# Down projection by seven block products, in three passes, with block additions on GpSimd

## The chip, the cores and the metric

The kernel runs on one core of one Trainium2 chip. The metric is the time of one execution in device microseconds (us). One execution in which every instruction was recorded (the profiled execution) gives the page, the groups and the time lines that are quoted. In the profile PE is the matrix engine (TensorE), PEld its weight loads, DVE is VectorE, ACT is ScalarE, POOL is GpSimd and SP is SyncE, which issues the DMAs here. PSUM is the memory into which PE writes its sums; it has eight banks of 128 partitions by 512 fp32 numbers.

## The reference

Two layers over 512 tokens of width 1024. Layer 0 mixes tokens by differential attention, layer 1 by gated linear attention (GLA), both beside a cross-attention into 256 memory tokens. Each layer ends in a gated MLP with a causal convolution of width 3 between its two projections, and this MLP is the part that the change rewrites:

```python
def conv_ffn(h, w_up, conv_w, conv_b, w_down):
    u = h @ w_up                       # 512 x 1024 by 1024 x 5632
    c = conv(u, width 3, causal, per column) + conv_b
    a, g = jnp.split(c, 2, axis=-1)
    return (jax.nn.silu(g) * a) @ w_down   # 512 x 2816 by 2816 x 1024

for i in range(DEPTH):                 # DEPTH = 2
    ...
    h = rms_norm(x, ffn_norm[i])
    x = x + conv_ffn(h, w_up[i], conv_w[i], conv_b[i], w_down[i])
```

## The kernel before

**Layout and precision.** Tokens are held transposed: `xT[k]` is one of eight tiles of 128 model columns by 512 tokens. A product in fp32 accuracy is made of three products in a faster format: each operand is split into a high part (ACT copies it, rounding) and a low part (DVE subtracts the high part), and PE sums high x high, high x low and low x high. `xh`, `xl` are the two parts of the tokens, `whi`, `wlo` those of the weights, `midh`, `midl` (or `xsh`, `xsl` in the buffers of the pool `xs`) those of the MLP's hidden tiles.

**Weights.** The host packs all weights into blocks of 128 x 1024 numbers in the order of their use. SP loads them through three `raw` buffers; `make_block` and `split_weights` (lines 251 and 254) split each into `whi` and `wlo`, of which there are six buffers (`WB`). `weights(key)` returns a piece's parts, and makes blocks up to two pieces ahead.

**The MLP.** `ffn` goes through the 11 groups of hidden columns (q, 256 columns of each half) in two passes, `HALVES = (6, 5)`. In a pass, `up` forms for every q four products (gate and value, two 128-column tiles of each), each of 24 matmuls of 512 tokens, in four PSUM banks with the tags mm and sm (two banks to a tag). The tokens are not yet divided by their root mean square there: the factor `rB` is found by `row_scales` while the first products run, and `conv` multiplies each product by it on DVE (line 1126), then applies the convolution with one ACT and two DVE instructions (1128 to 1130). Silu, a product and the split of the hidden tile follow (1161 to 1165). At the end of a pass, four steps c follow, each with the down projection for two output tiles, 2c and 2c+1: 36 or 30 matmuls of 512 tokens to a tile, in one bank of tag lg and one of tag tp. `update` adds the bank to `xT` (line 1074), and in layer 0's last pass makes the next layer's operands at once (line 309 on DVE, 308 on ACT) and sums up their squares (421, 423).

**Order.** PE's order is written by hand. The orders of the other engines are set by a scheduler when the program is built; each engine then takes its instructions strictly in that order, and waits on semaphores. The first projection of layer 1 (`gemm` with the key `gm`, lines 328 to 330) follows the last down projection of layer 0 on PE. It opens its first two sums in banks with the tag mm.

Of the kernel before, what the change touches and what calls it, by code (L numbers as in the profile page):

```python
# [21 lines left out]
S = 512  # L22
# [8 lines left out]
HALVES = (6, 5)  # L31
# [147 lines left out]
def trunk(ctx, tc, head_d, x_t, mem_t, wpack, cols_a_d, cols_d, conv_d, gate_d, rel_bias, diff_lambda, consts, onehot, out):  # L179
# [93 lines left out]

    def make_block(raws=None):
# [9 lines left out]
        hi, lo = (wp.tile([128, WTILE], F32R, name=t, tag=t, bufs=WB) for t in ("whi", "wlo"))  # L284
        split_weights(slice(0, n * w), raw, hi, lo, i == 2)
        made[i] += [(hi[:, blk(j, w)], lo[:, blk(j, w)]) for j in range(n)]
# [3 lines left out]
    used = [0]  # L290
# [820 lines left out]
    def ffn(pool, l, acc):  # L1111
        rB = pool.tile([128, S], F32, name="rB", bufs=1)
        us = [pool.tile([128, S + 128], F32, name=f"u{i}", bufs=1)[:, :S + 2] for i in range(4)]
        for u in us:
            G.memset(u[:, 0:2], 0.0)
        nu = [0]

        def up(parts, n):
            i = nu[0]
            nu[0] += 1  # L1120
            p = bank("mm" if i % 4 < 2 else "sm")
            product(p, parts, n, list(zip(xh, xl)))
            return p, us[i % 4]

        def conv(p, u, j):
            V.tensor_mul(u[:, 2:], p, rB)  # L1126
            c = pool.tile([128, S], F32, name="cvo", bufs=6)
            A.activation(c, u[:, 2:], AF.Identity, scale=cv[l][:, 2, j:j + 1], bias=cv[l][:, 3, j:j + 1])  # L1128
            V.scalar_tensor_tensor(c, u[:, 1:S + 1], cv[l][:, 1, j:j + 1], c, op0=ALU.mult, op1=ALU.add)  # L1129
            V.scalar_tensor_tensor(c, u[:, 0:S], cv[l][:, 0, j:j + 1], c, op0=ALU.mult, op1=ALU.add)  # L1130
            return c
# [15 lines left out]
        base = 0  # L1147
        for half, nq in enumerate(HALVES):
            mids = []
            for q in range(base, base + nq):  # L1150
                wa = weights(("ua", l, q))
                wg = None
                for n in range(2):
                    ua = up(wa, n)
                    wg = wg or weights(("ug", l, q))
                    ug = up(wg, n)
                    if q == 0 and n == 0:
                        row_scales(acc[0])
                    ca = conv(*ua, 2 * q + n)
                    cg = conv(*ug, 22 + 2 * q + n)  # L1160
                    A.activation(cg, cg, AF.Silu)
                    V.tensor_mul(ca, ca, cg)
                    mh, ml = split_tiles() if len(mids) < 5 else split_tiles(pool, "mid", 18)
                    A.copy(mh, ca)
                    V.tensor_sub(ml, ca, mh.bitcast(F32))
                    mids.append((mh, ml))
            last = half == 1
            if last and l == 0:
                tables("natural_log_exp_and_others")
            acc2 = [None]  # L1170
            for c in range(4):
                if last and l == 0 and c == 0:
                    gw = gate_raw[0] = pool.tile([128, S], F32, name="cvo", bufs=6)[:96, :384]
                    G.memset(gw, 0.0)
                    for b in range(3):
                        load(gw[32 * b:32 * b + 17], gate_d)
                pn = bank("lg"), bank("tp")
                parts = weights(("dn", l, base, c))
                final = last and l == 1 and c == 3
                for n in range(2):  # L1180
                    cut = len(parts) - 2 if final and n else len(parts)
                    product(pn[n], parts[:cut], n, mids)
# [102 lines left out]
```

## Time and profile before

| | us |
|---|---|
| time, median of 3 executions | 1163.88 |
| lowest and highest of the 3 | 1163.66, 1164.11 |
| time of the profiled execution | 1163.96 |
| its span, first to last instruction | 1162.2 |
| of the span: up and down stages of layer 0's MLP, about | 250 to 600 |
| of the span: up and down stages of layer 1's MLP, about | 808 to 1162 |

The span is 1.8 us shorter than the time of the same execution, since the time also holds what lies around the first and the last instruction. A matmul's record (389 ns for 512 tokens) is its way from its first input to its last output; matmuls overlap, so a matmul's price is the distance from its start to the next one's start. In the rows, `out<-in` names what is written and read, `xN` is a count, and a row of a group ends with the busy time, the mean length of one in ns, and the engine's idle time just ahead of them, with what ended that.

### The profile page before, as it was taken

What the parts mean: (1) busy time and instruction counts of PE and PEld (TensorE: products, weight loads), DVE (VectorE), ACT (ScalarE), POOL (GpSimd) and SP (SyncE); (2) the same over time, 40 slices, a digit from 0 to 9 for tenths busy, and PEclk for the clock granted to TensorE, in tenths of its full rate; (3) what the DMA queues carried; (4) which work ended last, traced back from release to release, by engine and by line L of the source; (5) the groups of instructions that cost most, each with busy time, mean ns of one, the idle gap of its engine ahead of it and who ended that gap; (6) DMA issues with size and microseconds to landing.
All of it is one profiled execution on the core that took longest, in us unless ns stands there. A gap on an engine that the chain in (4) does not pass through costs nothing.

```text
span 1162.2 us, 14796 instructions
## 1 busy us (share of the span) xinstructions
PE 1157.9 (100%) x5654; PEld 965.8 (83%) x5654; DVE 753.3 (65%) x1262; ACT 545.0 (47%) x951; POOL 6.5 (1%) x30
## 2 busy tenths in 40 slices
PE   9999999999999999999999999999999999999998
PEld 7888887888888888888888888988888888888887
DVE  8676778688677326677457737867976733576741
ACT  6677686555354213354337634436544421344420
POOL 0000000000000000000000000000000000000000
PEclk9999999999999999999999999999999999999999
DMA  8522242233223223222341320332332323232221
GB/s 295 166 82 83 78 144 70 73 108 128 73 93 125 88 80 124 73 98 94 121 146 66 98 96 8 119 112 104 106 112 73 106 94 109 88 112 73 90 101 45
DMA packets 39652, 117.70 MB, mean 101 GB/s; under 512 B 4767, under 2 KB 7256, under 8 KB 39582
## 3 DMA queue, kind: packets, MB, share of 16 engines
q1 hardware_dynamic: 39150, 116.37, 29.8%
q8 instruction: 44, 0.72, 0.3%
q10 hardware_dynamic: 432, 0.39, 0.1%
q14 instruction: 26, 0.21, 0.1%
HBM read 112.54 MB, written 4.21 MB: 100 GB/s over the span
## 4 chain that ended last, share of the span: by engine, by line
PE 99%; DMA 0%; DVE 0%; ACT 0%; issue 0%
PE ps_mm L350 9%; PE ps_mm L349 9%; PE ps_mm L351 9%; PE ps_sm L350 8%; PE ps_sm L351 8%; PE ps_sm L349 8%; PE ps_mm L328 6%; PE ps_mm L330 6%; PE ps_mm L329 6%; PE ps_lg L350 3%; PE ps_lg L351 3%; PE ps_lg L349 3%; PE ps_tp L350 3%; PE ps_tp L351 3%; PE ps_tp L349 3%; PE ps_tp L218 3%
## 5 line engine op out<-in xcount | busy, mean ns | idle before, releaser
L251 ACT CAST whi<-raw 128x1024 fp32r<-128x1024 f32 (+4 forms) x212 | 207.8, 986 | 257.1 <-PE ps_tp L350 120.9
L254 DVE TENSOR_TENSOR wlo<-raw,whi 128x1024 fp32r<-128x1024 f32 (+4 forms) x212 | 240.4, 1139 | 125.8 <-ACT whi L251 125.0
L349 PE MATMUL ps_mm<-xsh,whi 128*128 128x512 f32 x438 | 171.5, 392 | 0.0
L350 PE MATMUL ps_mm<-xsl,whi 128*128 128x512 f32 x438 | 170.6, 389 | 0.0
L351 PE MATMUL ps_mm<-xsh,wlo 128*128 128x512 f32 x438 | 170.5, 389 | 0.0
L349 PE MATMUL ps_sm<-xsh,whi 128*128 128x512 f32 x378 | 147.0, 389 | 0.0
L350 PE MATMUL ps_sm<-xsl,whi 128*128 128x512 f32 x378 | 147.0, 389 | 0.0
L351 PE MATMUL ps_sm<-xsh,wlo 128*128 128x512 f32 x378 | 147.0, 389 | 0.0
L328 PE MATMUL ps_mm<-whi,xsh 128*128 128x512 f32 (+2 forms) x328 | 126.4, 385 | 0.0
L1128 ACT ACTIVATE cvo<-u,cv 128x512 f32<-128x512 f32 x88 | 71.4, 815 | 111.8 <-DVE u L1126 111.8
L330 PE MATMUL ps_mm<-whi,xsl 128*128 128x512 f32 (+2 forms) x328 | 123.0, 375 | 0.0
L329 PE MATMUL ps_mm<-wlo,xsh 128*128 128x512 f32 (+2 forms) x328 | 122.8, 374 | 0.0
L349 PEld LDWEIGHTS ps_mm<-xsh,whi 128*128 128x128 f32 x438 | 82.2, 188 | 17.2 <-issue 0.3
L350 PEld LDWEIGHTS ps_mm<-xsl,whi 128*128 128x128 f32 x438 | 82.3, 188 | 17.1 <-DVE xsl L309 0.4
L351 PEld LDWEIGHTS ps_mm<-xsh,wlo 128*128 128x128 f32 x438 | 82.2, 188 | 17.1
L1129 DVE SCALAR_TENSOR_TENSOR cvo<-u,cv,cvo 128x512 f32<-128x512 f32 x88 | 65.7, 748 | 36.2 <-ACT cvo L1128 36.0
L349 PEld LDWEIGHTS ps_sm<-xsh,whi 128*128 128x128 f32 x378 | 71.0, 188 | 14.8
L350 PEld LDWEIGHTS ps_sm<-xsl,whi 128*128 128x128 f32 x378 | 71.0, 188 | 14.7
L351 PEld LDWEIGHTS ps_sm<-xsh,wlo 128*128 128x128 f32 x378 | 71.0, 188 | 14.6
L328 PEld LDWEIGHTS ps_mm<-whi,xsh 128*128 128x128 f32 x328 | 61.7, 188 | 11.5 <-issue 1.0
L330 PEld LDWEIGHTS ps_mm<-whi,xsl 128*128 128x128 f32 x328 | 61.7, 188 | 11.4
L329 PEld LDWEIGHTS ps_mm<-wlo,xsh 128*128 128x128 f32 x328 | 61.8, 188 | 10.0
(325 smaller groups left out, 1779.2 us busy)
## 6 DMA issues: line engine op xcount, KB each, us to landing
raw<-in_wpack_dram SPq DMA_DIRECT2D x178, 512.0 KB, 3.4
xt<-in_x_t_dram SPq DMA_DIRECT2D x15, 256.0 KB, 5.3
raw<-in_wpack_dram SPq DMA_DIRECT2D x15, 256.0 KB, 5.3
raw<-in_wpack_dram SPq DMA_DIRECT2D x8, 384.0 KB, 3.8
xres<-xt SPq DMA_DIRECT2D x8, 256.0 KB, 3.0
xt<-xres SPq DMA_DIRECT2D x8, 256.0 KB, 5.5
out_dram<-xt SPq DMA_DIRECT2D x7, 256.0 KB, 2.0
bt<-bias_d SPq DMA_DIRECT2D x6, 256.0 KB, 4.6
```

The costliest lines, as they stand in the source:

```text
L218: nc.tensor.transpose(dst, src, ident[:n, :n])
L251: ins = A.copy(hi[:, c], raw[:, c])
L254: V.tensor_sub(lo[:, c], raw[:, c], hi[:, c].bitcast(F32))
L328: mm(p, sh[k][:, blk(b)], hi, start=k == 0, stop=False)
L329: mm(p, sh[k][:, blk(b)], lo, start=False, stop=False)
L330: mm(p, sl[k][:, blk(b)], hi, start=False, stop=k == KT - 1)
L349: mm(p, hi[:, blk(n)], bh, start=i == first, stop=False)
L350: mm(p, hi[:, blk(n)], bl, start=False, stop=False)
L351: mm(p, lo[:, blk(n)], bh, start=False, stop=i == last)
L1128: A.activation(c, u[:, 2:], AF.Identity, scale=cv[l][:, 2, j:j + 1], bias=cv[l][:, 3, j:j + 1])
L1129: V.scalar_tensor_tensor(c, u[:, 1:S + 1], cv[l][:, 1, j:j + 1], c, op0=ALU.mult, op1=ALU.add)
```

## The change

The down projection is done by Strassen's scheme (in the form of Winograd). Two hidden tiles, two output tiles and two halves of the tokens make a 2 x 2 by 2 x 2 product of blocks, for which 7 block products do in place of 8. Each is of 128 x 128 weights by 256 tokens, with the three parts as before. For this, sums of weight blocks (`combined`, four additions to a block of weights) and sums of token halves (`combine`, four additions to a q) are formed on GpSimd (`ADD = G`) and split by ACT and DVE as the plain ones are; the seven products go to four banks, and `decode` puts the output tiles together from them on DVE. The passes become three, of 4, 4 and 3 groups q. Two steps c hold all eight banks in turn: one step has the tags mm and sm, the next lg and tp. From the third group on (q >= 2), the up projection reads tokens that are already scaled (`scaled_tokens`: on DVE, ACT and DVE, eight tiles, once in a layer), so that the multiplication by `rB` falls away, and ACT and DVE read the convolution's input from PSUM. The up stage takes its banks over all four tags (`TURNS`).

```diff
-HALVES = (6, 5)
+HALVES = (4, 4, 3)
+TURNS = ('mm', 'mm', 'sm', 'sm', 'lg', 'lg', 'tp', 'tp')
...
+    def combined(raw, n):
...
+        ADD.tensor_add(s1, a21, a22)
+        ADD.tensor_sub(s3, a11, a21)
+        ADD.tensor_sub(s2, s1, a11)
+        ADD.tensor_sub(s4, a12, s2)
+        A.copy(full(h0)[:, :, :3], r[:, :, :3])
+        V.tensor_sub(full(l0)[:, :, :3], r[:, :, :3], full(h0)[:, :, :3].bitcast(F32))
+        m = slice(0, 512 * pairs)
+        A.copy(h1[:, m], wsum[:, m])
+        V.tensor_sub(l1[:, m], wsum[:, m], h1[:, m].bitcast(F32))
...
+    ADD = G
...
+        if i + 1 < len(plan) and plan[i + 1][0][0] == "dn":
+            limit = first_of[i + 1] + 1
...
-        def conv(p, u, j):
-            V.tensor_mul(u[:, 2:], p, rB)
-            c = pool.tile([128, S], F32, name="cvo", bufs=6)
-            A.activation(c, u[:, 2:], AF.Identity, scale=cv[l][:, 2, j:j + 1], bias=cv[l][:, 3, j:j + 1])
...
+        def conv(p, j, scaled):
+            if not scaled:
+                u = ctile()
+                V.tensor_mul(u, p, rB)
+                p = u
+            c = ctile()
+            A.activation(c, p, AF.Identity, scale=cv[l][:, 2, j:j + 1], bias=cv[l][:, 3, j:j + 1])
+            V.scalar_tensor_tensor(c[:, 1:], p[:, :S - 1], cv[l][:, 1, j:j + 1], c[:, 1:], op0=ALU.mult, op1=ALU.add)
+            V.scalar_tensor_tensor(c[:, 2:], p[:, :S - 2], cv[l][:, 0, j:j + 1], c[:, 2:], op0=ALU.mult, op1=ALU.add)
...
+        def scaled_tokens():
+            out = []
+            for k in range(KT):
+                t = ctile()
+                V.scalar_tensor_tensor(t, xT[k], c_ffn(l, k), rB, op0=ALU.mult, op1=ALU.mult)
+                hi, lo = split_tiles()
+                A.copy(hi, t)
+                V.tensor_sub(lo, t, hi.bitcast(F32))
+                out.append((hi, lo))
+            return out
...
+        def combine(b2, b1):
+            t12, t34 = ctile(), ctile()
+            ADD.tensor_sub(t12[:, left], b1[:, right], b1[:, left])
+            ADD.tensor_sub(t12[:, right], b2[:, right], t12[:, left])
+            ADD.tensor_sub(t34[:, left], b2[:, right], b1[:, right])
+            ADD.tensor_sub(t34[:, right], b2[:, left], t12[:, right])
+            h, lo, m = (mid_tile(), mid_tile()), (mid_tile(), mid_tile()), mid_tile()
+            parts_of(b1[:, left], m[:, left], m[:, right])
+            for t, hi, lw in zip((t12, t34), h, lo):
+                parts_of(t, hi, lw)
...
+        def down(base, nq, mids, tags, last, acc2):
...
+            two = 2 if nq == 4 else 1
+            seq = [(0, m) for m in range(nq - 1)] + [(1, m) for m in range(two)] + [(0, nq - 1)]
+            seq += [(1, m) for m in range(two, nq)] + [(c, m) for c in (2, 3) for m in range(nq)]
...
+                ta, tb = (("mm", "sm"), ("lg", "tp"))[(c + tags) % 2]
+                banks[c] = [bank(t) for t in (ta, ta, tb, tb)]
...
+                for t, (w, v) in enumerate(((hi, bh), (hi, bl), (lo, bh))):
+                    mm(banks[c][b][:, h], w, v, start=b not in seen[c], stop=m == nq - 1 and t == 2 and i in close)
...
+            def decode(c):
+                n1, n2, b = 2 * c, 2 * c + 1, banks[c]
+                u = ctile()
+                x1, x2 = xT[n1], xT[n2]
+                A.copy(u[:, left], b[2][:, left])
+                V.tensor_add(x1[:, left], x1[:, left], b[2][:, left])
+                V.tensor_add(u[:, left], u[:, left], b[2][:, right])
+                V.tensor_add(u[:, right], u[:, left], b[1][:, right])
+                V.tensor_add(u[:, left], u[:, left], b[3][:, left])
+                V.tensor_add(x1[:, right], x1[:, right], u[:, right])
+                x2v = x2.rearrange("p (h c) -> p h c", h=2)
+                V.tensor_add(x2v, x2v, u[:, left].unsqueeze(1).to_broadcast([128, 2, 256]))
...
+                x1, x2, b = decode(c)
+                V.tensor_add(x2, x2, b[1])
+                finish_tile(2 * c + 1)
...
+                    V.tensor_add(x1, x1, b[0])
+                    finish_tile(2 * c)
...
+            for q in range(base, base + nq):
+                if q == 2:
+                    tokens = fresh
...
+                if q == 0:
+                    fresh = scaled_tokens()
```

The orders below are those of the built programs. Line numbers in the rows of the change are those of the changed kernel.

**PE, at the border of the layers.** The end of layer 0's last down projection (lines 349 to 351 before, 1257 in the change) and the start of layer 1's first projection (328 to 330 before, 364 to 366 in the change; `128x272` is its width). Before:

```order
L349 MATMUL ps_tp<-midh,whi 128x512
L350 MATMUL ps_tp<-midl,whi 128x512
L351 MATMUL ps_tp<-midh,wlo 128x512
L328 MATMUL ps_mm<-whi,xsh 128x272
L329 MATMUL ps_mm<-wlo,xsh 128x272
```

And in the change:

```order
L1257 MATMUL ps_sm<-mid,whi 128x256 x2
L1257 MATMUL ps_sm<-mid,wlo 128x256
L1257 MATMUL ps_mm<-mid,whi 128x256 x2
L1257 MATMUL ps_mm<-mid,wlo 128x256
L364 MATMUL ps_mm<-whi,xsh 128x272
L365 MATMUL ps_mm<-wlo,xsh 128x272
```

The last sums of layer 0 moved from the banks lg and tp to mm and sm, so that layer 1's first sum asks for a bank that the last step of the down projection has just filled.

**DVE, at the same place.** Before, the last step's two additions to `xT` (1074), each with the low part (309) and the squares (423) of a next operand, and low parts of weights (254):

```order
L1074 TENSOR_TENSOR xt<-xt,ps_lg 128x512
L309 SCALAR_TENSOR_TENSOR xsl<-xt,cols_a,xsh 128x512
L423 TENSOR_TENSOR xt<-xt 128x512
L254 TENSOR_TENSOR wlo<-raw,whi 128x1024 x2
L1074 TENSOR_TENSOR xt<-xt,ps_tp 128x512
L254 TENSOR_TENSOR wlo<-raw,whi 128x1024
```

In the change, from the step before the last (banks lg and tp) to the last one (mm and sm); 1265 to 1271 are `decode`, 1313 and 1306 the additions behind it, 345 and 459 the next operand and its squares, 257 low parts of weights:

```order
L1313 TENSOR_TENSOR xt<-xt,ps_lg 128x512
L1306 TENSOR_TENSOR xt<-xt,ps_lg 128x512
L257 TENSOR_TENSOR wlo<-raw,whi 128x1024
L345 SCALAR_TENSOR_TENSOR xsl<-xt,cols_a,xsh 128x512
L459 TENSOR_TENSOR xt<-xt 128x512
L345 SCALAR_TENSOR_TENSOR xsl<-xt,cols_a,xsh 128x512
L459 TENSOR_TENSOR xt<-xt 128x512
L257 TENSOR_TENSOR wlo<-raw,whi 128x1024
L1265 TENSOR_TENSOR xt<-xt,ps_sm 128x256
L1266 TENSOR_TENSOR cvo<-cvo,ps_sm 128x256
L1267 TENSOR_TENSOR cvo<-cvo,ps_mm 128x256
L1268 TENSOR_TENSOR cvo<-cvo,ps_sm 128x256
```

A step now has eight additions on DVE in place of two, the step before it and two blocks of layer 1's weights stand ahead of the last step's, and the bank mm is read last (line 1313 of the last step, a few rows further on).

**DVE, between the first and the third group q of a layer.** Before, the work of one q after another:

```order
L254 TENSOR_TENSOR wlo<-raw,whi 128x1024
L1162 TENSOR_TENSOR cvo<-cvo 128x512
L1126 TENSOR_TENSOR u_2662<-ps_sm,rB 128x512
L254 TENSOR_TENSOR wlo<-raw,whi 128x1024
L1165 TENSOR_TENSOR xsl<-cvo,xsh 128x512
```

In the change, with the scaled tokens (1192) and their low parts (1195), and the multiplications by `rB` of q = 1 (1166):

```order
L1192 SCALAR_TENSOR_TENSOR cvo<-xt,cols,rB 128x512
L1195 TENSOR_TENSOR xsl<-cvo,xsh 128x512
L1192 SCALAR_TENSOR_TENSOR cvo<-xt,cols,rB 128x512
L1166 TENSOR_TENSOR cvo<-ps_lg,rB 128x512
L1195 TENSOR_TENSOR xsl<-cvo,xsh 128x512
L1166 TENSOR_TENSOR cvo<-ps_lg,rB 128x512
L1195 TENSOR_TENSOR xsl<-cvo,xsh 128x512
L1170 SCALAR_TENSOR_TENSOR cvo<-cvo,cv_81 128x511
L257 TENSOR_TENSOR wlo<-raw,whi 128x1024
```

Sixteen instructions for the scaled tokens now stand ahead of most of q = 1's work and of the low parts of the weights of q = 2 (line 257).

More of the change, by code (lines that the diff above doesn't have):

```diff
@@ L283, in make_block @@
             made.append([])
-        hi, lo = (wp.tile([128, WTILE], F32R, name=t, tag=t, bufs=WB) for t in ("whi", "wlo"))
-        split_weights(slice(0, n * w), raw, hi, lo, i == 2)
-        made[i] += [(hi[:, blk(j, w)], lo[:, blk(j, w)]) for j in range(n)]
+        if plan[i][0][0] == "dn":
+            made[i] += combined(raw, n)
+        else:
+            hi, lo = (wp.tile([128, WTILE], F32R, name=t, tag=t, bufs=WB) for t in ("whi", "wlo"))
+            split_weights(slice(0, n * w), raw, hi, lo, i == 2)
+            made[i] += [(hi[:, blk(j, w)], lo[:, blk(j, w)]) for j in range(n)]
         if raws is None:
             ahead()
-    used = [0]
+    used, sum_pool = [0], [None]
+    ADD = G
     def weights(key, by_block=False):
@@ L1197, in ffn @@
+                gw = gate_raw[0] = ctile()[:96, :384]
+                G.memset(gw, 0.0)
+                for b in range(3):
+                    load(gw[32 * b:32 * b + 17], gate_d)
+            down(base, nq, mids, nu[0] // 4 % 2, last, acc2)
             base += nq
```

160 lines of the change are left out of this document (111 added, 49 removed).

## The prediction

> **What bounds the kernel now.** The page comes first: busy shares, the granted clock, the chain of waits.
>
> ```profile
> span 1162.2 us, 14796 instructions
> PE 1157.9 (100%) x5654; PEld 965.8 (83%) x5654; DVE 753.3 (65%) x1262; ACT 545.0 (47%) x951; POOL 6.5 (1%) x30
> ...
> PEclk9999999999999999999999999999999999999999
> ...
> PE 99%; DMA 0%; DVE 0%; ACT 0%; issue 0%
> ```
>
> PE ends nearly everything: the chain is 99% PE, and PE is never long without a matmul. So a matmul taken away is time gained, at once, and any wait of PE is time lost, at once; DVE and ACT count only where they make PE wait. How much room they have is read stage by stage, in the busy time by windows: the first and the second group q of layer 0's up stage, then a quarter of a down stage (columns: window, its length, then busy time and count of PE, PEld, DVE, ACT, POOL).
>
> ```profile
> 251.50:273.20 21.70, 21.70 (x97) 18.00 (x96) 19.47 (x27) 12.81 (x16) 0.00 (x0) 1.00 0.28 97
> 273.20:294.90 21.70, 21.70 (x97) 17.96 (x97) 16.02 (x21) 9.65 (x12) 0.00 (x0) 1.00 0.29 98
> 388.50:405.00 16.50, 16.50 (x75) 13.65 (x74) 5.14 (x6) 3.34 (x4) 0.00 (x0) 1.00 0.28 95
> ```
>
> DVE has 2.2 us left in the first q, 5.7 in the next, and two thirds of the down stage. The change puts its additions into that room.
>
> **What the change takes from PE.** The down projection is these groups by form, of line 349, and as many of 350 and 351:
>
> ```profile
> L349 PE MATMUL ps_lg<-midh,whi 128*128 128x512 f32 x96 | 37.4, 389 | 0.0
> L349 PE MATMUL ps_tp<-midh,whi 128*128 128x512 f32 x94 | 36.6, 389 | 0.0
> L349 PE MATMUL ps_lg<-xsh,whi 128*128 128x512 f32 x80 | 31.1, 389 | 0.0
> L349 PE MATMUL ps_tp<-xsh,whi 128*128 128x512 f32 x80 | 31.1, 389 | 0.0
> ```
>
> That is 3 x 350 = 1050 matmuls of 512 tokens, and 12 of 256 at the very end. The distance of starts comes from the time line, the first and the last of 42 in a row of 512 tokens, and of 22 in a row of 256:
>
> ```profile
> 1147.87 0.39 PE L349 MATMUL ps_lg<-xsh,whi 128*128 128x512 f32 x1
> ...
> 1157.16 0.39 PE L351 MATMUL ps_tp<-midh,wlo 128*128 128x512 f32 x1
> ```
>
> ```profile
> 738.74 0.28 PE L330 MATMUL ps_mm<-whi,xsl 128*128 128x256 f32 x1
> ...
> 741.25 0.28 PE L330 MATMUL ps_mm<-whi,xsl 128*128 128x256 f32 x1
> ```
>
> 9.29 us / 41 = 0.2266 and 2.51 / 21 = 0.1195, so a half-width matmul costs 53% of a full one. Before: 1050 x 0.2266 + 12 x 0.1195 = 239.4 us. After: 11 pairs of hidden tiles x 4 pairs of output tiles x 7 products x 3 parts x 2 layers = 1848 matmuls, x 0.1195 = 220.8. **Gain 18.6 us**, not the eighth (30 us) that seven for eight suggests.
>
> **What DVE is given.** Its prices, by form (the mean in ns is the second number behind the bar):
>
> ```profile
> L254 DVE TENSOR_TENSOR wlo<-raw,whi 128x1024 fp32r<-128x1024 f32 x178 | 216.7, 1222 | 120.1 <-ACT whi L251 119.4
> L254 DVE TENSOR_TENSOR wlo<-raw,whi 128x816 fp32r<-128x816 f32 x2 | 2.0, 1009 | 2.3 <-ACT whi L251 2.3
> L254 DVE TENSOR_TENSOR wlo<-raw,whi 128x768 fp32r<-128x768 f32 x8 | 7.5, 953 | 1.0 <-ACT whi L251 1.0
> L254 DVE TENSOR_TENSOR wlo<-raw,whi 128x512 fp32r<-128x512 f32 x15 | 10.3, 685 | 0.0
> L254 DVE TENSOR_TENSOR wlo<-raw,whi 128x256 fp32r<-128x256 f32 x8 | 3.3, 418 | 2.3 <-ACT whi L251 2.2
> L309 DVE SCALAR_TENSOR_TENSOR xsl<-xt,cols_a,xsh 128x512 fp32r<-128x512 f32 x8 | 6.0, 750 | 3.8 <-ACT xsh L308 3.8
> L423 DVE TENSOR_TENSOR xt<-xt 128x512 f32<-128x512 f32 x31 | 21.2, 685 | 0.3
> L1126 DVE TENSOR_TENSOR u<-ps_mm,rB 128x512 f32<-128x512 f32 x44 | 30.1, 688 | 35.6 <-PE ps_mm L351 35.5
> ```
>
> An addition of 256 numbers is put at 0.42, of 512 at 0.69, from PSUM or not; 384 and 544 lie between at 0.55 and 0.72. Then a step c costs DVE 5 x 0.42 + 3 x 0.69 = 4.2 us where two additions cost 1.4.
>
> *Layer 0's last pass (three groups), the main loss.* PE's work there is 4 x 63 x 0.1195 = 30.1 us. DVE, from the last gate product of the up stage to the addition that frees the bank mm, by the rows of its order and the prices above: that product and the low parts of the last hidden tiles 2.5; three whole steps 12.5 and the fourth up to that addition 3.5; next operands and squares of three steps 7.9; down weights, now 1.75 times as wide for the block sums, 8.1; weights for layer 1, two of 816, one of 544, three of 1024, 6.4. Sum 40.9. Neighbouring records overlap, and there are waits:
>
> ```profile
> 600.30 1.23 DVE L254 TENSOR_TENSOR wlo<-raw,whi 128x1024 fp32r<-128x1024 f32 x1 [1.50 <-ACT whi L251]
> 601.45 0.68 DVE L1074 TENSOR_TENSOR xt<-xt,ps_tp 128x512 f32<-128x512 f32 x1
> 602.04 1.22 DVE L254 TENSOR_TENSOR wlo<-raw,whi 128x1024 fp32r<-128x1024 f32 x1
> 603.18 0.75 DVE L309 SCALAR_TENSOR_TENSOR xsl<-xt,cols_a,xsh 128x512 fp32r<-128x512 f32 x1
> ```
>
> Overlap is 0.08 an instruction here, some 4 us over 60 of them; waits as these (1.5 on ACT) may add 4. So 37 to 45 us, and they begin about 4 us behind PE, after the last product's convolution (one ACT pass, two DVE passes, Silu):
>
> ```profile
> L1128 ACT ACTIVATE cvo<-u,cv 128x512 f32<-128x512 f32 x88 | 71.4, 815 | 111.8 <-DVE u L1126 111.8
> L1161 ACT ACTIVATE cvo<-cvo 128x512 f32<-128x512 f32 x44 | 27.7, 629 | 44.9 <-DVE cvo L1130 44.7
> ```
>
> The bank mm is free 41 to 49 us after the pass began, and PE is done at 30 to 33. Before, PE ran straight through this border, since the banks differed:
>
> ```profile
> 600.34 0.39 PE L351 MATMUL ps_tp<-midh,wlo 128*128 128x512 f32 x1
> 600.56 0.28 PE L328 MATMUL ps_mm<-whi,xsh 128*128 128x272 f32 x1
> ```
>
> The projection needs the bank before its first matmul, and behind it in PE's order waits all of layer 1. **Loss 8 to 17 us, taken as 13.** Even with DVE idle the last decode alone would cost 3.5.
>
> *The third group q, twice.* Scaled tokens are 8 x (0.75 + 0.69) = 11.5 us of DVE; low parts for 1792 columns of a q in place of 1024 add 1.1 each. The first two q then need 19.5 + 16.0 + 2.2 + 11.5 = 49.2 us of DVE in PE's 43.4, and the weights' and tokens' low parts that q = 2 reads stand behind most of it. Loss between 2 (part of q = 1's work may come later) and 8 (5.8, and the 2.2 of idle time that the first q could not use); taken as 4 in each layer, **8 together**. From q = 2 on, four multiplications (2.8) fall away against 1.1 added, and DVE recovers.
>
> *In the other passes* DVE has 4 x (4.2 + 4.3) = 34 us for PE's 40, and in layer 1's last pass no next operands: no loss.
>
> **GpSimd.** No two-input operation of it is in the trace. The nearest rows:
>
> ```profile
> L474 POOL CAST oh<-oh_raw 64x640 fp32r<-64x640 f32 x1 | 0.7, 712 | 14.8 <-DMA oh_raw<-in_onehot_dram 14.8
> L1115 POOL MEMSET u<- 128x2 f32 x8 | 0.4, 101 | 270.2 <-PE ps_tp L218 177.1 <-DVE wlo L254 93.1
> ```
>
> Some 0.1 fixed and 0.95 ns for an element of one input. With 256 elements: 0.35 if both inputs come at once, 0.6 if one after the other; 0.6 is taken, 1.2 is the far end (double again). 280 of them are 170 us in 700, so their amount is hidden. Their delay is not where the cover is short: in a last pass PE does three pairs (7.5 us) before it needs the last q's combined tiles, and these come after 4 us of convolution, 0.7 of product, three GpSimd steps (1.8), ACT 0.6 and DVE 0.7, together 7.8 and a fourth step behind. Loss 0 to 4 in each layer, taken as 1.5, **3 together**. In passes of four groups PE has five pairs (12.5 us): hidden.
>
> A shared resource: if a two-input instruction of DVE stood still while GpSimd reads, DVE would lose up to 170 us over the two MLPs; if they do not touch, nothing. No row has both at work. I take **3 us** of PE time, near the lower end, as DVE has room in most stages. The Trainium skill (GPSIMD Engine Reference, Key points) speaks against the change here: GpSimd shares its SBUF interfaces with VectorE, with contention against instructions with two SBUF inputs, as nearly all these are; no run here shows it yet, and by it the third case below holds.
>
> **The tail.** Before, the last matmul began at 1158.70, and 3.5 us later all was out; now an addition and a DMA follow it again, but DVE may be behind by part of a step: 0 to 3, **1.5**.
>
> ```profile
> 1158.70 0.28 PE L351 MATMUL ps_sm<-midh,wlo 128*128 128x256 f32 x1
> 1159.02 0.42 DVE L1189 TENSOR_TENSOR xt<-xt,ps_sm 128x256 f32<-128x256 f32 x1 [0.22 <-PE ps_sm L351]
> ```
>
> **Sum**, against the profiled execution's span: 1162.2 - 18.6 + 13 + 8 + 3 + 3 + 1.5 = 1172.1. The time of that execution was 1163.96, 1.8 above its span, and the median of the runs (1163.88) is the same to 0.1; so 1173.9, say **1174 us**. A clock that falls while PE waits is not in it: the trace has PEclk 9 in every slice. By the Trainium skill (TensorE: Matmul & The Clock Gate, The HAM clock gate) an idle window of about 3.4 us halves the clock until about as long a busy one; after the long wait that would be 1.7 us more, 1175.6, an estimate from that page.
>
> **The rivals.**
> 1. *DVE stays hidden* (faster). If layer 1's first projection waited only for the last decode (3.5), and q = 2, the hidden tiles and the tail for nothing, the time is 1164 - 18.6 + 3.5 = 1149. For it: DVE is idle 35% of the span. Against it: the idle time is not in the last pass, where 41 us of work stand against 30.
> 2. *The waits just eat the gain*: 16 to 21 us of them, 1162 to 1166. It needs the lower ends at the border (8) and at q = 2 (4), with 4 to 9 for the rest.
> 3. *GpSimd and DVE slow each other.* If each GpSimd operation holds DVE for its second read, 0.25 us, that is 70 us more on DVE, a tenth of the MLPs' time; at q = 2 and at the border the lag then grows by a tenth of 49 and of 41 us, 14 in all with both layers, and last hidden tiles come 2 later in each: 1174 + 18 = 1192. It decides once DVE's room in a q (some 7 us of 21.7) no longer covers the lag carried over.
> 4. *The weight load sets the pace*: a load's record is 188 ns, and 1848 of these would be 347 us, a loss of 108, 1290 with the waits. Against it: the 256-wide rows above run at 0.1195 with a load each.
>
> ```profile
> L349 PEld LDWEIGHTS ps_mm<-xsh,whi 128*128 128x128 f32 x438 | 82.2, 188 | 17.2 <-issue 0.3
> ```
>
> **How the numbers follow.** Forecast (waits of 22 to 38, 1167 to 1183) 0.62, rival 1 0.10, rival 2 0.07, rival 3 0.20, rival 4 0.01. 0.2% of the time, 2.3 us, is about what a measurement of this kernel tells from no change. Rival 2 is split: 0.05 within it, 0.02 faster. Slower: 0.62 + 0.20 + 0.01 = 0.83; same 0.05; faster 0.12. The range reaches from 1164, where the lower bounds meet, to 1194, above rival 3.
>
> **What would show it.** The chain of waits of the changed kernel: PE waits once for 8 to 17 us at layer 1's first projection, released by DVE's line 1313; twice for 2 to 8 us at q = 2, released by DVE (257 or 1195); PE's starts 0.12 apart in the down stage; GpSimd's mean near 0.6 us. I am wrong if PE passes the border without a wait, if DVE's 256-wide additions are far from 0.42, or if a 256-wide matmul with its own weights takes more than 0.13.

## The result and the profile after

| | before | after |
|---|---|---|
| median of 4 runs each, us | 1163.91 (1163.66 to 1164.11) | 1189.95 (1189.53 to 1191.63) |
| ratio, 95% interval | | 1.0227 [1.0209, 1.0244] |
| profiled execution / its span, us | 1163.96 / 1162.2 | 1190.02 / 1188.2 |

The change costs 26.0 us of span where 9.9 were forecast. The page of the changed kernel, in the lines that were shown of the one before (in the last two, each digit is one fortieth of the span):

```profile
span 1188.2 us, 17113 instructions
PE 1150.6 (97%) x6440; PEld 995.8 (84%) x6440; DVE 885.9 (75%) x1473; ACT 612.5 (52%) x1083; POOL 264.3 (22%) x302
...
POOL 0000000001780146313600000000146403370353
PEclk9999999999999999999979999999999999999999
...
PE 87%; DVE 8%; POOL 1%; issue 1%; ACT 1%; DMA 1%; DVEq 0%; ACTq 0%; POOLq 0%
```

PE is no longer the whole chain: 8% of it is DVE. GpSimd's 264 us look like little (22%), but the row by slices shows that they come in six clumps whose fullest slice is busy to 50 to 80%, each around the start of a down stage. What PE waited for (total us, number of waits, longest):

```profile
PE ps_mm L364 <- DVE xt L1313: 12.9, 1, 12.9
PE ps_mm L1257 <- DVE xt L1313: 7.5, 5, 1.9
PE ps_mm L387 <- DVE wlo L257: 6.0, 2, 3.3
PE ps_tp L1257 <- ACT mid L1205: 2.9, 2, 1.4
PE ps_tp L1257 <- DVE mid L1206: 2.4, 3, 1.8
```

Line 364 is the border of the layers: one wait of 12.9 us for the bank. Line 387 is q = 2, once in each layer. Lines 1205 and 1206 are the last hidden tiles. The second row is the one that the prediction had said would not be there: in a down stage, step c = 2 finds its banks still waiting for the last addition of step c = 0. Four of these five waits, 6.7 us, are in the passes of four groups, and one of 0.85 us is in layer 0's pass of three.

Half clock adds to it. Windows of 3.41 us (length, PE's busy time and count, granted clock, DMA share, GB/s), each pair a window and the one behind it; at the border, from 609 us, three windows and the fourth:

```profile
353.41:356.83 3.42, 1.84 (x15) 1.00 0.00 0
356.83:360.24 3.41, 3.41 (x31) 1.00 0.51 154
578.70:582.11 3.41, 1.54 (x10) 1.00 0.07 21
582.11:585.52 3.41, 3.41 (x18) 0.50 0.01 2
609.42:619.66 10.24, 0.88 (x4) 0.50 0.54 189
619.66:623.07 3.41, 3.41 (x17) 0.50 0.35 136
872.24:875.66 3.42, 0.21 (x1) 1.00 0.00 0
875.66:879.07 3.41, 3.41 (x9) 0.50 0.65 171
1155.55:1158.96 3.41, 1.64 (x13) 1.00 0.52 154
1158.96:1162.38 3.42, 3.42 (x15) 0.50 0.00 0
```

In four windows PE had work and ran it at half clock (18 matmuls of 256 in place of 31). Each costs half of 3.41 us: 6.8 us.

The spacing of matmuls in an undisturbed step (first and last row of 27 periods of three matmuls), and the tail:

```profile
484.50 0.28 PE L1257 MATMUL ps_mm<-mid,wlo 128*128 128x256 f32 x1
...
494.21 0.28 PE L1257 MATMUL ps_tp<-mid,wlo 128*128 128x256 f32 x1
...
1182.88 0.28 PE L1257 MATMUL ps_mm<-mid,wlo 128*128 128x256 f32 x1
```

9.71 us / 81 = 0.1199 from one start to the next, so PE's gain is 239.4 - 1848 x 0.1199 = 17.8 us. From the last matmul's start to the end of the span 5.3 us pass, where the kernel before takes 3.5. Each wait should also cost a little beyond its length (an estimate from these records): the last matmul ahead of it takes its whole 0.28 us where the next would have started after 0.12, so 0.16 us for each of 13 waits.

| term, us | predicted | measured |
|---|---|---|
| PE's matmuls | -18.6 | -17.8 |
| border of the layers | 13 | 12.9 |
| q = 2 | 8 | 6.0 |
| last hidden tiles | 3 | 2.9 + 2.4 = 5.3 |
| GpSimd and DVE in each other's way, seen as bank waits in the down stages | 3 and 0 | 7.5 |
| half clock | 0 | 6.8 |
| tail | 1.5 | 1.8 |
| running dry at 13 waits (estimate) | 0 | 2.1 |
| sum / span's change | 9.9 | 24.6 / 26.0 |

No term was found for the last 1.4 us.

**How the two engines meet.** In layer 0's first down stage the time line of the changed kernel alternates (start, length; first two additions with DVE idle, then a stretch with both at work):

```profile
335.32 0.74 POOL L287 TENSOR_TENSOR wsum<-raw 128x256 f32<-128x256 f32 x1
336.02 0.74 POOL L288 TENSOR_TENSOR wsum<-wsum,raw 128x256 f32<-128x256 f32 x1
...
348.19 0.74 POOL L286 TENSOR_TENSOR wsum<-raw 128x256 f32<-128x256 f32 x1
348.21 1.53 DVE L291 TENSOR_TENSOR wlo<-raw,whi 128x768 fp32r<-128x768 f32 x1
...
348.89 1.45 POOL L287 TENSOR_TENSOR wsum<-raw 128x256 f32<-128x256 f32 x1
349.67 1.75 DVE L294 TENSOR_TENSOR wlo<-wsum,whi 128x1024 fp32r<-128x1024 f32 x1
```

The addition of line 286 ends at 348.93. DVE's subtraction began at 348.21, was 0.95 long in the kernel before, and ends at 349.74, 0.81 after GpSimd's end. GpSimd's next addition, 0.74 alone, began at 348.89 and ends at 350.34, 0.60 after DVE's end; DVE's next, 1.22 alone, ends at 351.42, 1.08 after GpSimd's. Each ends 0.14 us less than its own length after the other's end: they take turns, instruction by instruction. The groups of the changed kernel (busy us, mean ns of one) say which instructions this touches:

```profile
L294 DVE TENSOR_TENSOR wlo<-wsum,whi 128x1024 fp32r<-128x1024 f32 x40 | 59.3, 1482 | 19.5 <-ACT whi L293 19.5
L1206 DVE TENSOR_TENSOR mid<-cvo,mid 128x512 fp32r<-128x512 f32 x66 | 52.2, 793 | 34.1 <-ACT mid L1205 33.0
L291 DVE TENSOR_TENSOR wlo<-raw,whi 128x768 fp32r<-128x768 f32 x40 | 43.5, 1087 | 6.8 <-ACT whi L290 6.4
L1313 DVE TENSOR_TENSOR xt<-xt,ps_lg 128x512 f32<-128x512 f32 x12 | 8.1, 678 | 0.0
L1212 POOL TENSOR_TENSOR cvo<-cvo 128x256 f32<-128x256 f32 x22 | 27.2, 1235 | 327.2 <-DVE cvo L1335 327.2
L289 POOL TENSOR_TENSOR wsum<-raw,wsum 128x256 f32<-128x256 f32 x40 | 44.7, 1118 | 3.1
```

The last addition to `xT` was, in the kernel before:

```profile
L1074 DVE TENSOR_TENSOR xt<-xt,ps_lg 128x512 f32<-128x512 f32 x16 | 11.0, 688 | 67.7 <-PE ps_lg L351 67.7
```

DVE's instructions with both inputs in SBUF (the memory in which tokens, weights and hidden tiles lie) are longer: 1482 ns for 1222, 793 for 690, 1087 for 953. An addition with one input in PSUM is not (line 1313, 678 for 688). GpSimd's additions of 256 take 0.74 to 1.24 us by line, and 0.6 was taken. Whether this is what makes the waits, the experiments had to tell.

### The profile page after: what moved, and what is told of

Its sections match the earlier page's. It is cut to its first block, busy times and chain, and to the rows that moved or that the text cites. A ratio compares the mean times of both kernels' runs of the same rounds, so it can differ in the third digit from the quotient of the medians.

```text
span 1188.2 us, 17113 instructions
## 1 busy us (share of the span) xinstructions
PE 1150.6 (97%) x6440; PEld 995.8 (84%) x6440; DVE 885.9 (75%) x1473; ACT 612.5 (52%) x1083; POOL 264.3 (22%) x302
## 4 chain that ended last, share of the span: by engine, by line
PE 87%; DVE 8%; POOL 1%; issue 1%; ACT 1%; DMA 1%; DVEq 0%; ACTq 0%; POOLq 0%
PE ps_mm L364 6%; PE ps_mm L366 6%; PE ps_mm L365 6%; PE ps_mm L387 5%; PE ps_mm L385 5%; PE ps_mm L386 5%; PE ps_mm L1257 4%; PE ps_sm L386 4%; PE ps_sm L385 4%; PE ps_sm L387 4%; PE ps_lg L1257 4%; PE ps_sm L1257 3%; PE ps_tp L1257 3%; PE ps_tp L385 3%; PE ps_lg L385 3%; PE ps_tp L387 3%
## 5 line engine op out<-in xcount | busy, mean ns | idle before, releaser
L364 PE MATMUL ps_mm<-whi,xsh 128*128 128x512 f32 (+2 forms) x328 | 127.4, 389 | 12.9 <-DVE xt L1313 12.9
L387 PE MATMUL ps_mm<-xsh,wlo 128*128 128x512 f32 x278 | 109.1, 392 | 6.0 <-DVE wlo L257 6.0
L385 PE MATMUL ps_mm<-xsh,whi 128*128 128x512 f32 x278 | 110.0, 396 | 0.0
L386 PE MATMUL ps_mm<-xsl,whi 128*128 128x512 f32 x278 | 108.9, 392 | 0.0
L1206 DVE TENSOR_TENSOR mid<-cvo,mid 128x512 fp32r<-128x512 f32 x88 | 66.5, 757 | 39.8 <-ACT mid L1205 38.6
L385 PE MATMUL ps_sm<-xsh,whi 128*128 128x512 f32 x218 | 84.8, 389 | 0.0
L386 PE MATMUL ps_sm<-xsl,whi 128*128 128x512 f32 x218 | 84.8, 389 | 0.0
L387 PE MATMUL ps_sm<-xsh,wlo 128*128 128x512 f32 x218 | 84.8, 389 | 0.0
L364 PEld LDWEIGHTS ps_mm<-whi,xsh 128*128 128x128 f32 x328 | 62.7, 191 | 24.6 <-issue 14.1
L294 DVE TENSOR_TENSOR wlo<-wsum,whi 128x1024 fp32r<-128x1024 f32 (+1 forms) x48 | 66.9, 1394 | 20.9 <-ACT whi L293 20.9
L1257 PE MATMUL ps_mm<-mid,whi 128*128 128x256 f32 x346 | 64.4, 284 | 7.5 <-DVE xt L1313 7.5
L1257 PE MATMUL ps_lg<-mid,whi 128*128 128x256 f32 x352 | 66.7, 287 | 0.0
```

The lines of the kernel that those rows point to most:

```text
L294: V.tensor_sub(l1[:, m], wsum[:, m], h1[:, m].bitcast(F32))
L364: mm(p, sh[k][:, blk(b)], hi, start=k == 0, stop=False)
L385: mm(p, hi[:, blk(n)], bh, start=i == first, stop=False)
L386: mm(p, hi[:, blk(n)], bl, start=False, stop=False)
L387: mm(p, lo[:, blk(n)], bh, start=False, stop=i == last)
L1206: V.tensor_sub(lo, t, hi.bitcast(F32))
```

## The experiments

Theory A: what costs is that DVE and GpSimd hold each other up. Theory B: DVE simply has too much to do. For the border, theory C: the bank is the wait; theory D: DVE's queue is.

**Additions on DVE.**

```
-    ADD = G
+    ADD = V
```

> All 280 block additions go from GpSimd to DVE. DVE takes 248 x 0.42 + 32 x 0.30 = 114 us more. Theory A (the two engines slow each other): DVE's instructions with two SBUF inputs fall back to their prices of before (1024 wide 1482 -> 1223 ns, 768 wide 1087 -> 955, 512 wide 793 -> 685), some 35 us less, and GpSimd's wait in the last hidden tiles (5.2 us, with 3 us of half clock behind it) falls to 2 or less: DVE's busy time about 965 us, span 1180 to 1192, no slower than the changed kernel. Theory B (DVE's own work decides, what GpSimd does to it is small): DVE keeps its prices of after, is 114 us busier (1000 us), and every wait on DVE grows: border 13 -> 20, bank waits in the passes of four 7.5 -> 15, q = 2 6 -> 10: span 1205 to 1215.

Measured: 1172.70 us, ratio to the kernel before 1.0074 [1.0057, 1.0091], span 1171.2. That is below theory A's interval and far below theory B's, and DVE's busy time (929.3 us) is below both figures. GpSimd has no additions left, DVE's subtractions are back at their old prices, and an addition takes DVE 0.42:

```profile
L294 DVE TENSOR_TENSOR wlo<-wsum,whi 128x1024 fp32r<-128x1024 f32 x40 | 48.9, 1222 | 11.0 <-ACT whi L293 11.0
L1206 DVE TENSOR_TENSOR mid<-cvo,mid 128x512 fp32r<-128x512 f32 x66 | 44.5, 682 | 1.5 <-ACT mid L1205 1.5
L289 DVE TENSOR_TENSOR wsum<-raw,wsum 128x256 f32<-128x256 f32 x40 | 16.8, 420 | 0.5
```

PE's waits, of which the border alone is left at full size:

```profile
PE ps_mm L364 <- DVE xt L1313: 13.4, 1, 13.4
PE ps_mm L387 <- DVE wlo L257: 2.8, 2, 1.4
PE ps_mm L1257 <- DVE xt L1313: 1.0, 1, 1.0
```

So DVE is busier in all (929.3 us for 885.9) and PE loses 17 us less. A stretch of 20 us of layer 0's first down stage, which begins at 331.7 in the changed kernel and at 330.0 in this one (columns as in the prediction's windows), first the changed kernel, then this one:

```profile
336.00:356.00 20.00, 18.09 (x151) 17.91 (x150) 17.43 (x19) 10.15 (x14) 19.61 (x19) 1.00 0.26 80
```

```profile
332.00:352.00 20.00, 20.00 (x169) 20.00 (x168) 18.77 (x37) 8.93 (x13) 0.00 (x0) 1.00 0.27 82
```

Beside 19 additions of GpSimd, DVE brings 19 instructions to an end; alone it does 37, additions included. GpSimd itself is full there, 19.61 of 20 us.

**No additions.** The products take the unsummed blocks:

```
-    ADD.tensor_add(s1, a21, a22)
...
+    wsum = raw
...
-    ADD.tensor_sub(t12[:, left], b1[:, right], b1[:, left])
...
+    t12, t34 = b1, b2
```

> The 280 additions are left out (products take the unsummed blocks, so the output is not the reference's); everything else of DVE, ACT and PE stays. Theory A (GpSimd stretches DVE, and that makes the waits in the passes of four): DVE's busy time falls by 30 to 40 us to about 850, the 7.5 us of bank waits in the passes of four go, the border falls from 12.9 to 8 to 10, q = 2 from 6 to 3, the last hidden tiles from 5.2 to 2, half clock from 6.7 to 3: span 1166 to 1172. Theory B (DVE's own work decides): only the last hidden tiles' wait and its half clock go (6 us): span 1181 to 1184, with the passes of four still at 7 and the border at 12.

Measured: 1164.75 us, ratio 1.0008 [0.9999, 1.0017], span 1162.2, 26.0 us below the changed kernel's. DVE's same 1473 instructions take 846.0 us in place of 885.9. The waits left:

```profile
PE ps_mm L359 <- DVE xt L1304: 12.6, 1, 12.6
PE ps_mm L382 <- DVE wlo L257: 0.7, 1, 0.7
PE ps_mm L1248 <- DVE xt L1304: 0.3, 1, 0.3
```

Theory A, and beyond it: the span is below its 1166 to 1172, and q = 2, put at 3, is at 0.7. The border is the exception; it was to fall to 8 to 10 and stayed. In that pass DVE is full even here, and while PE waits DVE works for 11.5 of 12.6 us:

```profile
580.00:585.00 5.00, 4.99 (x42) 4.79 (x40) 5.00 (x11) 2.93 (x5) 1.15 (x3) 1.00 0.44 116
...
592.00:604.60 12.60, 0.09 (x1) 0.12 (x1) 11.47 (x20) 4.37 (x6) 0.00 (x0) 0.64 0.69 239
```

So the border has little to do with GpSimd. It also shows how little the change could give with its additions for nothing: PE's 17.8 us, less 13.6 of waits, 1.7 of half clock behind the border, 1.8 of tail and 0.5 of running dry, leave 0.2.

**Additions made, but read by nobody.** GpSimd does all its work, and nothing reads a result of it:

```
-    A.copy(h1[:, m], wsum[:, m])
+    A.copy(h1[:, m], raw[:, m])
...
-    for t, hi, lw in zip((t12, t34), h, lo):
+    for t, hi, lw in zip((b1, b2), h, lo):
```

> GpSimd makes all 280 additions, but nothing reads them: the products take the unsummed blocks, so the output is not the reference's. Against the kernel without additions (span 1162.2) only GpSimd's use of the memory ports comes back, and no engine waits for its results. Theory A (the two engines slow each other): DVE's instructions with two SBUF inputs are as long as in the changed kernel (1024 wide over 1400 ns, 512 wide over 750), the passes of four wait 5 to 8 us, q = 2 3 to 6: span 1173 to 1182. Theory I (what costs is the wait for GpSimd's results): 1162 to 1166.

Measured: 1187.69 us, ratio 1.0210 [1.0194, 1.0226], span 1185.4: 23.2 of the 26.0 us between the changed kernel and the one without additions come back, above the 1173 to 1182 that theory A had asked for. DVE's 1473 instructions take 899.3 us where they took 846.0 without additions:

```profile
L1206 DVE TENSOR_TENSOR mid<-cvo,mid 128x512 fp32r<-128x512 f32 x66 | 63.3, 967 | 0.6 <-ACT mid L1205 0.4
L294 DVE TENSOR_TENSOR wlo<-raw,whi 128x1024 fp32r<-128x1024 f32 x40 | 59.2, 1480 | 21.3 <-ACT whi L293 21.2
```

```profile
PE ps_mm L1257 <- DVE xt L1313: 7.9, 5, 2.0
PE ps_mm L387 <- DVE wlo L257: 5.4, 2, 2.8
```

**The same, with the raw weights let go early.** One rival was left: GpSimd's additions hold buffers. They hold the tile of raw weights, and so delay the next load; and in the run with unread additions ACT still waited three times, 7.1 us in all, for GpSimd to be done with a buffer. Here k1 and k2 are constants, and three of the four additions in `combine` read constants in the same way.

```
-    ADD.tensor_sub(s3, a11, a21)
-    ADD.tensor_sub(s2, s1, a11)
-    ADD.tensor_sub(s4, a12, s2)
+    ADD.tensor_sub(s3, k1, k2)
+    ADD.tensor_sub(s2, s1, k2)
+    ADD.tensor_sub(s4, k1, s2)
```

> As the run with unread additions (1185.4 us of span, output not the reference's), but only the first of each four additions reads the weights or the hidden tile; the other three add constants. So GpSimd lets go of a buffer of raw weights after one addition, not after four, and works as much as before. Theory A (what costs is that both engines read SBUF): DVE's instructions with two SBUF inputs stay long (1024 wide over 1400 ns), span 1180 to 1187. Rival J (what costs is that GpSimd's slow chain holds the raw weights and delays their loads and copies): the bank waits of 7.9 us and q = 2's 5.4 go for the most part, span 1165 to 1174.

Measured: 1187.92 us, ratio 1.0203 [1.0186, 1.0220], span 1184.9. DVE's subtractions stay long (1437 ns at 1024 wide, 983 at 512), and ACT no longer waits for GpSimd. Theory A; the rival falls. One thing is not held fixed: DVE's built order differs a little between the kernel without additions and the one with unread ones (1399 of 1473 places hold the same instruction), so some of the 23.2 us may be order. The longer instructions are not.

**Only the hidden tiles' 88 additions on DVE**, the weights' 192 still on GpSimd (`ADD` becomes `V` in the function `combine` alone).

> Only the additions of the hidden tiles (88) go to DVE, those of the weights (192) stay on GpSimd. If the chain of four GpSimd additions is what the last hidden tiles wait for, their 5.2 us and the 3.2 us of half clock behind them fall under 1. If the stretch comes from the weights' additions in the down stages, the bank waits in the passes of four stay at 6 to 8 us: span 1179 to 1182. If it comes as much from the hidden tiles' additions in the up stages, q = 2 falls from 6.0 to under 3 as well, and the passes of four to 4: span 1173 to 1177.

Measured: 1175.98 us, ratio 1.0104 [1.0090, 1.0118], span 1174.4, the last of the three cases. q = 2 falls to 2.8, the last hidden tiles to 0.8, the bank waits of the down stages only to 4.7. So the smaller lot of additions, those of the hidden tiles, costs 13.8 of the 17 us, and the weights' 3.2. A likely reason, which no run isolates, is that they fall where the hidden tile that PE wants next is made.

**The banks' turn shifted in layer 0.**

```
-    nu[0] = 0
+    nu[0] = 4 if l == 0 else 0
```

> In layer 0 the turn of the PSUM banks is shifted by one, so that the last step c = 3 of the down projection uses lg and tp and layer 1's first projection finds mm free. Theory C (the bank is the wait, as the prediction had it): the border's 12.9 us fall to 3 to 5, with half clock 2 us less: span 1176 to 1180. Theory D (DVE's queue is the wait: the projection's operands of the last two tiles come from the same queue, one instruction before and two after the addition that frees the bank): 10 to 13 us stay, now at a later matmul or released by the operand's low part (line 336): span 1185 to 1190.

Measured: 1185.08 us, ratio 1.0181 [1.0163, 1.0199], span 1183.3, between the two theories. The border's one wait is now four, of 2.9, 1.3, 0.8 and 0.4 us, the second and fourth for operands:

```profile
PE ps_mm L364 <- DVE xt L1313: 2.9, 1, 2.9
PE ps_mm L364 <- ACT xsh L344: 1.3, 1, 1.3
```

The bank was more than half of the wait, and behind it stand the operands of the last tiles from the same queue. The span falls by 4.9 us, less than the border's waits (7.5): PE now works through two windows of half clock at the border where it was one, and through two at layer 1's q = 2, where it was one as well. **Shift and additions on DVE together:**

> Additions on DVE, and the shifted turn of the banks in layer 0. With the banks shifted under GpSimd's additions the span fell by 4.9 us, the border's waits from 12.9 to 5.3 in four pieces. Theory C (bank and queue are both waits in a row, whichever engine adds): again 4 to 6 us, span 1165 to 1168. Theory D (DVE now has 11 us more to do in that pass, so the operands come later still): less than 2 us, span 1169 to 1172.

Measured: 1166.75 us, ratio 1.0024 [1.0014, 1.0035], span 1165.0, 6.2 less than with DVE's additions alone: theory C, at the better end of its interval.

**No scaled tokens.**

```
-    if q == 2:
-        tokens = fresh
...
-    ca = conv(ua, 2 * q + n, q > 1)
...
+    ca = conv(ua, 2 * q + n, False)
...
-    if q == 0:
-        fresh = scaled_tokens()
```

> No scaled tokens: every group q is multiplied by rB after its product, as the first two are; 11.5 us of DVE work fall away ahead of q = 2 in each layer, and 9 x 2.8 us are added over the later groups. Theory E (the 11.5 us are what q = 2 waits for): its waits of 2.75 and 3.26 us go, with 1.5 us of half clock: span 1180 to 1183, if DVE has room for 2.8 us in each later q. Rival F (DVE has no such room beside GpSimd): the lag moves into the down stages, bank waits in the passes of four grow from 7.5 to 12 or more: span 1187 to 1195.

Measured: 1206.60 us, ratio 1.0368 [1.0353, 1.0384], span 1203.8. The waits at q = 2 do go, and theory E was right in that alone; the time was in neither interval. The bank waits stay at 7.8, but those for the last hidden tiles (lines 1205 and 1206) grow from 5.3 to 17.0 us, now in every pass, with half clock behind them. Two things have changed for each product. It goes through one more instruction of DVE before its convolution; and the two DVE instructions of the convolution now read from SBUF alone, where the changed kernel reads PSUM from the third group on and they take 743 to 748 ns:

```profile
L1171 DVE SCALAR_TENSOR_TENSOR cvo<-cvo,cv 128x510 f32<-128x510 f32 x88 | 75.4, 858 | 2.8
L1170 DVE SCALAR_TENSOR_TENSOR cvo<-cvo,cv 128x511 f32<-128x511 f32 x88 | 72.8, 828 | 22.4 <-ACT cvo L1169 22.1
```

So beside GpSimd's additions the scaled tokens pay for themselves, but the run does not tell how much of that is the saved instruction and how much the longer ones.

**PE kept busy at the border**, with additions on DVE:

```
+    if last and l == 0:
+        p = bank("lg")
+        for t in range(84):
+            mm(p[:, left], mids[0][0][0][:, :128], mids[0][1][0], start=t == 0, stop=t == 83)
```

> Additions on DVE (span 1171.2, with a wait of 13.4 us at the border and 17.1 us of half clock), and in that wait 84 matmuls of 256, 10 us, into the bank lg, which is free some 2 us after PE's last product; nothing reads them. Theory K (the granted clock follows how busy PE was just before): the half clock shrinks to one stretch of 3.4 us or none, and most of the 2.6 us that matmuls lost to it come back: span 1168.5 to 1170. Rival L (the loss after the wait is the restart, not the clock): 1171 or more.

Measured: 1170.33 us, ratio 1.0049 [1.0034, 1.0064], span 1168.8, 2.4 less than without: ten us of useless matmuls have made the program shorter. The clock is at half for 3.4 us in place of 17.1, and the mean granted clock is 0.998 for 0.992: theory K.

**Eight products in layer 0's last pass**, additions on DVE:

```
+    plain = l == 0 and base == 8
...
-    down(base, nq, mids, nu[0] // 4 % 2, last, acc2)
+    if plain:
+        plain_down(base, mids, acc2)
+    else:
+        down(base, nq, mids, nu[0] // 4 % 2, last, acc2)
```

Here `plain_down` is the loop over c of the kernel before.

> Additions on DVE, and layer 0's last pass multiplies its three groups as the kernel before does (eight products, the banks lg and tp, one addition for each output tile). Theory G (DVE's amount of work in that pass, 41 us against PE's 30, makes the border's wait): the 13.4 us and about 4 us of half clock and restart behind them go, and 3/11 of one layer's gain comes back, 17.4 / 2 x 3 / 11 = 2.4 us: span 1171.2 - 17.4 + 2.4 = 1156, within 1154 to 1159, faster than before by 0.4 to 0.8%. Rival H (layer 1's first projection waits for its operands whatever DVE did before): 5 us or more stay at the border, span 1161 or more.

Measured: 1158.73 us, ratio 0.9960 [0.9948, 0.9973], span 1156.5: theory G, the border's wait is gone. A wait of 1.4 us for the last hidden tile is new. The edit changes two things at once, DVE's work in that pass and the banks (lg and tp in place of mm and sm). The run with the shifted banks tells them apart: the banks alone took the border's waits from 13.4 to 5.9 us (2.9 + 2.0 + 1.0), and the rest goes with the work.

**Scaled tokens in two halves**, used from q = 3, and the first plain step in an order that needs the last hidden tiles later:

```
-    fresh = scaled_tokens()
+    fresh = scaled_tokens(fresh, range(4 * q, 4 * q + 4))
...
+    for ids in (range(4), range(4, 6)) if c == 0 else (range(6),):
```

> Additions on DVE and the plain last pass of layer 0 (span 1156.5), with two more edits. The scaled tokens are made in two parts, four after q = 0 and four after q = 1, and used from q = 3; and the first step of the plain pass multiplies all but its last two hidden tiles for both outputs first. If the q = 2 waits (1.44 and 1.33) come from 11.5 us of DVE at one place, and the wait for the last hidden tile (1.43 and 0.22) from too little cover, all four go: span 1152 to 1154. Rival: DVE's 2.8 us more in q = 2 turn up as waits elsewhere: 1156 or more.

Measured: 1154.16 us, ratio 0.9910 [0.9895, 0.9924], span 1152.5; all four waits are gone, the two at q = 2 and the two for the last hidden tile of the plain pass. **And layer 1's last pass plain too:**

> As the run before, and layer 1's last pass is plain as well. It gives up 2.4 us of gain and takes away three waits (0.34, 0.67, 0.22) and the longer tail (5.3 us from the last matmul's start to the end, where the kernel before has 3.5): within 1 us of the run before, 1151 to 1154. Rival: the plain pass brings waits of its own, as it did in layer 0 (1.65): 1155 or more.

Measured: 1152.66 us, ratio 0.9897 [0.9882, 0.9912], span 1150.4, just under its interval and faster than both kernels:

```profile
span 1150.4 us, 16395 instructions
PE 1145.6 (100%) x6230; PEld 983.4 (85%) x6230; DVE 876.2 (76%) x1598; ACT 596.2 (52%) x1047; POOL 6.1 (1%) x22
...
PE 97%; DVE 2%; issue 0%; ACT 0%; ACTq 0%
```

Eight of the eleven groups give 8/11 x 17.8 = 12.9 us; 11.8 arrive.

## Why the prediction was right and wrong

**The direction and the border held.** PE's gain (17.8 for 18.6), the border (12.9 for 13), its releaser (DVE's line 1313) and the tail (1.8 for 1.5) are as worked out. The cause given for the border, DVE's 41 us in a pass of 30, is shown from two sides. It stands without GpSimd's additions: there the bank is free 43.4 us after the pass's first product and PE is done after 30.9, both inside what was forecast (41 to 49 and 30 to 33). And it goes in two parts: with the additions on DVE 7.5 us go with other banks, and the rest goes when the pass asks less of DVE. In the changed kernel both ends came later (50.1 and 37.2), so their difference was met in part by luck. Weight loads do not set the pace, 0.1199 between matmuls.

**q = 2 was near in size, but not by its mechanism.** The 8 us were worked out from DVE's own work alone. With that work and without the additions the waits at q = 2 are 0.7 us, with the additions on DVE 2.8, with GpSimd's 6.0: most of the 6.0 belongs to GpSimd. The scaled tokens are the other condition, as these waits go without them.

**The step that failed is GpSimd's.** The prediction wrote "280 of them are 170 us in 700, so their amount is hidden", and of the shared resource "I take 3 us of PE time, near the lower end, as DVE has room in most stages". Both argue from a mean over stages with different limits. The additions come in clumps where DVE is full: there GpSimd was busy 19.61 us of 20, and DVE brought 19 instructions to an end where it does 37 alone. The two terms were 3 us each; without the additions the span is 26.0 us shorter, and 23.2 of these stand when nothing reads the sums. An addition's price was mis-sized as well: 0.74 us with DVE idle for the 0.6 taken. From this step come three of the misses in the table: the bank waits of the down stages ("no loss", 7.5; 0.3 without additions), the last hidden tiles (5.3 for 3; none without), and most of the half clock (one window of work in place of four).

**The third rival was the answer**, its 1192 us beside the measured 1190, and it had a chance of 0.20. It named the mechanism, two engines that hold each other up, with a price of the right order (70 us more on DVE; 885.9 - 846.0 = 39.9 were measured). But it sent the loss to q = 2, the border and the last hidden tiles alone: the border did not grow by it (12.6 without additions, 12.9 with them), and the bank waits and the half clock were not in it. That its time came so near is in part luck. What should have raised its chance stood in the prediction as the rule of the Trainium skill (GPSIMD Engine Reference, Key points), which the trace now bears out, and the bounds of the cost, nothing to 170 us. A value near the lower end had no row behind it. The Trainium skill (SBUF — State Buffer, SBUF: two separate sides) goes further and calls the shared pair "an **exclusive lock**, not a bandwidth split"; the turns at 348 us, each instruction ending 0.14 us less than its own length after the other's end, agree.

**The sum was near the kernel without that mechanism.** With additions on DVE the span is 1171.2, and the sum was 1172.1. In part that is luck: the border is 13.4, q = 2 only 2.8, half clock and running dry make up for it.

**The clock was left out of the sum.** The prediction reckoned 1.7 us after the one long wait; that window cost 1.7, half of 3.41. The other three came after waits of 1.4 to 3.3 us, and the prediction had none of them in view.

**Two bounds do not follow from their own figures.** A bank free after 41 to 49 us and PE done at 30 to 33 give a loss of 8 to 19 at the border, not 8 to 17; and the lower bounds of the waits (8 and 4, the others nothing) give 1157, not the 1164 at which the range begins. Neither bears on the step that failed.

## What to carry over

Before work is moved to an idle engine, look at what it shares with the busy one, and at the stage in which it will run, not at its mean over the span: here, where both were at work, an addition on GpSimd held DVE for 0.5 to 0.6 us, and DVE does it in 0.42. Over all 280 it was only 39.9 / 280 = 0.14 us each, so it is the stage that decides. A scheme that saves products and adds additions belongs in the stages in which the adding engine has room; with the additions on DVE, the scaling spread out and the scheme left out of the two short passes, a loss of 2.3% became a gain of 1.0%. And in the changed kernel PE's waits cost a second time, 1.7 us, in each of the four windows of work that ran at half clock behind them.

## What was not expected of the hardware

In these traces the granted clock goes by fixed windows, not by the length of a wait. In the traces of all the kernels here every stretch between two changes of the clock, but for the ends of the program, is a whole number of 3.413 us: in the changed kernel 1, 7, 4, 74, 1, 82, 1 and 7 of them. In the changed kernel a window in which PE was busy for 1.54, 0.21 or 1.64 us was followed by one at half clock, one with 1.84 us was not, so that a limit would lie between 48 and 54% there. It is the window that counts: a wait of 2.75 us at 296 us, split over two windows, cost no clock, and two of 1.4 and 0.3 us in one window did.

Two other traces narrow the limit: a window with 1.67 us was not followed by half clock with the banks shifted in layer 0 (at 352.83), nor with the hidden tiles' additions on DVE (at 597.65). But the kernel without scaled tokens does not fit: windows with 2.28 and 2.05 us (at 475.69 and 1062.78) were followed by half clock. PE's busy share in the records is not all that counts, and what else does stays open.

The Trainium skill (TensorE: Matmul & The Clock Gate, The HAM clock gate) has the window free-running and 3.413 us long, which agrees; it speaks of idle windows, and two of those in the changed kernel were almost half busy (1.54 and 1.64 us of 3.41).
